# First gated input: order of sigmoids and forms, place of the third FFN's first weights, and block order of its first pair

## The chip, the cores and the metric

The kernel runs on one core of one Trainium2 chip. The metric is device time in microseconds; the median of three runs before the change is 2196.75 us (2195.62 to 2200.46). The engines in the profile are PE (matmuls) with PEld (its weight loads), DVE (VectorE), ACT (ScalarE), POOL (GpSimd) and SP (SyncE, which issues the weights' DMAs).

## The reference

Two layers act on a stream h of 512 tokens by 1024 features. Each layer runs a half-step SwiGLU FFN, a token mixer (retention in layer 0, forgetting attention in layer 1), a second half-step FFN, and a gated per-layer input; each takes a normed copy of h.

```
for i in range(DEPTH):
    h = h + 0.5 * swiglu(rmsnorm(h, nw[0]), ffn_w_in[i, 0], ffn_w_out[i, 0])
    hn = rmsnorm(h, nw[1])
    h = h + (retention(hn, ...) if i % 2 == 0 else forgetting_attention(hn, ...))
    h = h + 0.5 * swiglu(rmsnorm(h, nw[2]), ffn_w_in[i, 1], ffn_w_out[i, 1])
    gate = jax.nn.sigmoid(rmsnorm(h, nw[3]) @ ple_w_gate[i])
    h = h + gate * (p[i] @ ple_w_proj[i])
return rmsnorm(h, final_norm_w)
```

All is float32. The change is at the gated input of layer 0 and at the first FFN of layer 1, which follows it (the third of four FFNs, ffn index 2).

## The kernel before

**Layout.** h lies transposed in eight blocks h[0..7] of 128 features by 512 tokens. A product in float32 is made of three matmuls of rounded operands (`mm3`): weight high part times input high part, high times low, low times high. A "split" makes the parts: ScalarE casts the high part (L82), and the engine `W.low` subtracts it from the raw value for the low part (L83); `W.low` is VectorE in the FFNs and GpSimd inside `ple` (the gated input).

**Weights.** `W.plan` lists all weight blocks in order of use. `take` emits blocks up to two ahead (LOOKAHEAD): a DMA on SP into one of four raw buffers (`wraw`), then the split into one of three slots (`w8`). A raw buffer is free when both parts are made, a slot when PE's last product with it is done.

**The FFN's input half.** It is computed by a scheme of 2 by 2 quarters with seven products (Strassen's), on pairs of weight blocks: `Pair.q` and `Pair.r`. Most pairs need sums of quarters of the weights (`emit_sums`: adds at L151, splits at L82 and L83, buffers s12, s34 and a12 in a pool that each FFN opens) and sums and differences of the normed input's quarters, the "forms" (`Norm.quarters`: L381 to L412, whose casts and low parts are at L376 and L377). The first two pairs (PLAIN) are done plainly, from weights without sums: `plain(0)` and `plain(1)`, with 96 matmuls each at L526, 8 blocks by 2 halves of the tokens by 2 outputs by 3. They need the four quarters b11, b21, b12 and b22 of the forms; b12 (the "corner", L305 and L306) is made only for these, in buffers that the gates' inputs leave free.

**The gated input, `ple(0, ...)`.** For each block m PE makes the gate (`gates`: 24 matmuls) and the projected input (`added`: 6). Then `rest(m)`: VectorE scales the gate by the rows (L1112), ScalarE takes the sigmoid (L1113), VectorE multiplies (L1116) and adds to h[m] (L1117), and `nxt.block(m)` makes the next norm's forms of block m and adds its square into `acc` (L428, L432). After block 7 the sum of squares is split (L302, L303), and PE adds it over the features (L326, after the first plain pair) for the norm's scale.

**What sets the order.** PE's instructions stand in program order. Those of the other engines are ordered ahead of time by a planner that goes by readiness in its own cost model and by program order among what is ready; on the chip each engine then runs its own list strictly in order. The small tiles (`tmp`) have seven buffers.

Of the kernel before, what the change touches and what calls it, by code (L numbers as in the profile page):

```python
# [54 lines left out]
class Weights:  # L55
# [3 lines left out]
    def __init__(self, tc, raw_pool, pool):  # L59
        self.tc, self.nc, self.raw_pool, self.pool = tc, tc.nc, raw_pool, pool  # L60
        self.plan, self.ready, self.used = [], [], 0
        self.low = self.nc.vector
        self.limit, self.spare = None, []
        self.sum_pool, self.open_ffn, self.pairs_used = None, None, 0
        self.ahead, self.behind = 0, ()

# [18 lines left out]
    def chunk(self, src):  # L85
        n = src.shape[1]
        raw = self.load(src)
        if self.spare:
            tiles = [self.spare.pop(0)() for _ in range(4)]
            for i in range(2):  # L90
                self.split(raw[:, 512 * i : 512 * (i + 1)], tiles[i], tiles[2 + i])
            return Halves(tiles[0:2]), Halves(tiles[2:4])
        t = self.pool.tile([P, 2, 1024], F32R, name="w8")
        self.split(raw[:, :n], t[:, 0, :n], t[:, 1, :n], src)
        return t[:, 0, :], t[:, 1, :]
# [46 lines left out]
    def emit_sums_now(self):  # L142
        nc = self.nc
        pairs = [p for p in self.plan[: len(self.ready)] if isinstance(p, Pair) and p.ffn == self.open_ffn]
        for pair in pairs[: self.pairs_used + self.ahead]:
            if hasattr(pair, "s"):
                continue
            a11, a22 = pair.raw[:, 0:512], pair.raw[:, 512:1024]
            raw = self.load(pair.r)
            a12, a21 = raw[:, 0:512], raw[:, 512:1024]  # L150
            add = lambda o, p, q: nc.vector.tensor_tensor(out=o, in0=p, in1=q, op=ALU.add)  # L151
            fresh = lambda: self.sum_pool.tile([P, 512], F32, name="sums", bufs=4)
            s1, s2, s3, s4 = fresh(), fresh(), fresh(), fresh()
            pair.s = [self.sum_pool.tile([P, 2, 512], F32R, name=n, bufs=3) for n in ("s12", "s12", "s34", "s34")]
            pair.x = self.sum_pool.tile([P, 2, 512], F32R, name="a12")
            add(s1, a21, a22)
            add(s2, s1, a11)
            self.split(s1, pair.s[0][:, 0, :], pair.s[0][:, 1, :])
            self.split(s2, pair.s[1][:, 0, :], pair.s[1][:, 1, :])
            add(s4, s2, a12)  # L160
            add(s3, a21, a11)
            self.split(s4, pair.s[3][:, 0, :], pair.s[3][:, 1, :])
            self.split(s3, pair.s[2][:, 0, :], pair.s[2][:, 1, :])
            self.negated(a12, pair.x[:, 0, :], pair.x[:, 1, :], pair.r[:, 0:512])

    def open(self, ffn, pool):
        self.open_ffn, self.sum_pool, self.pairs_used, self.ahead, self.behind = ffn, pool, 0, 0, ()

    def begin(self, behind):
        self.ahead, self.behind = 2, behind  # L170
        self.emit_sums()
        self.behind = ()

    def take(self, src):
        assert self.plan[self.used] is src
        self.emit(self.used + 1 + LOOKAHEAD)
        self.used += 1
        return self.ready[self.used - 1]

# [8 lines left out]
def trunk(ctx, tc, a):  # L188
# [144 lines left out]
    class Norm:  # L333
        def __init__(self, gain, *pools):
            self.gain, self.hi, self.lo, self.acc = gain, [], [], None
            self.free = [p for p, n in pools for _ in range(n)]
            self.forms = [] if len(self.free) >= 28 else None
            self.new, self.left, self.extra = True, KB, None

        def unit(self):  # L340
            return unit(self.free.pop(0))
# [27 lines left out]
        def quarters(self, b):  # L369

            f = lambda ap: ap.bitcast(F32)
            c0, c1 = HALVES
            g = self.gain[:, b : b + 1]

            def part(raw, hi, lo, c):
                nc.scalar.copy(hi[:, c], raw[:, c])  # L376
                nc.vector.tensor_tensor(out=lo[:, c], in0=raw[:, c], in1=f(hi[:, c]), op=ALU.subtract)  # L377

            if b % 2 == 0:
                e, t = temp(), temp()  # L380
                nc.scalar.activation(e, h[b], AF.Identity, scale=g)  # L381
                if b // 2 == len(self.forms):
                    u = self.unit()
                    nc.scalar.copy(u[:, c0], e[:, c0])
                    nc.vector.tensor_tensor(out=u[:, c1], in0=e[:, c0], in1=f(u[:, c0]), op=ALU.subtract)
                    self.forms.append({"b11": (u[:, c0], u[:, c1])})
                ah, al = self.unit(), self.unit()
                nc.vector.tensor_tensor(out=t[:, c0], in0=e[:, c0], in1=e[:, c1], op=ALU.subtract)
                part(t, ah, al, c0)
                self.now = e, t, ah, al  # L390
                self.forms[b // 2].update({"t1": (ah[:, c0], al[:, c0]), "t2": (ah[:, c1], al[:, c1])})
            else:
                form = self.forms[b // 2]
                e, t, ah, al = self.now
                o, v = temp(), temp()
                nc.scalar.activation(o, h[b], AF.Identity, scale=g)
                if "b21" not in form:
                    oh, ol = self.unit(), self.unit()
                    part(o, oh, ol, slice(0, S))
                    form.update(b21=(oh[:, c0], ol[:, c0]), b22=(oh[:, c1], ol[:, c1]))  # L400
                if b == KB - 1 and self.extra:
                    for j, x in enumerate(self.forms):
                        u = unit(self.extra)
                        x["b12"] = u[:, c0], u[:, c1]
                        split(h[2 * j][:, c1], *x["b12"], self.gain[:, 2 * j : 2 * j + 1])
                nc.vector.scalar_tensor_tensor(
                    out=t[:, c1], in0=t[:, c0], scalar=-1.0, in1=o[:, c1], op0=ALU.mult, op1=ALU.subtract
                )
                part(t, ah, al, c1)
                bh, bl = self.unit(), self.unit()  # L410
                nc.vector.tensor_tensor(out=v[:, c0], in0=o[:, c1], in1=e[:, c1], op=ALU.subtract)
                nc.vector.scalar_tensor_tensor(  # L412
                    out=v[:, c1], in0=t[:, c1], scalar=-1.0, in1=o[:, c0], op0=ALU.mult, op1=ALU.subtract
                )
                part(v, bh, bl, slice(0, S))
                form.update(t3=(bh[:, c0], bl[:, c0]), t4=(bh[:, c1], bl[:, c1]))

        def square(self, b, ts_=slice(0, S), keep=False):

# [83 lines left out]
    def ffn(i, n, nxt, stack, apool, meanwhile=None):  # L503
# [7 lines left out]
        def plain(m, between=None):  # L511
# [1 line left out]
            ws = [W.take(ins[m].q), W.take(ins[m].r)]  # L513
            g, u = bank(), bank()
            order = [(k, t) for k in range(KB) for t in range(2)]
            if i:
                order.sort(key=lambda kt: kt[1])
            for at, (k, t) in enumerate(order):
                if at == 10 and between:
# [73 lines left out]

        done = PLAIN[i]
        whole = [plain(m) for m in range(done - 1)]
        W.begin(n.columns())

        def scaled():
            n.rows()
# [470 lines left out]
    def ple(l, n, nxt, phi, plo, parts=1):  # L1070

        w = S // parts
        with ExitStack() as pools:
# [12 lines left out]
            for part in range(parts):  # L1086
# [15 lines left out]
                def added(m):  # L1102
# [4 lines left out]
                        mm3(o, wp[0][:, ks], wp[1][:, ks], phi[k][:, ts_], plo[k][:, ts_], k == 0, k == 1)  # L1107
                    return o

                def rest(m, g, o):  # L1110
                    t1, t2, hm = temp()[:, :w], temp()[:, :w], h[m][:, ts_]
                    nc.vector.tensor_tensor(out=t1, in0=g, in1=n.r[:, ts_], op=ALU.mult)  # L1112
                    nc.scalar.activation(t1, t1, AF.Sigmoid)  # L1113
                    if parts > 1 and m == KB - 1:
                        nc.scalar.activation(warm, t1[:, 0:1], AF.Sqrt)
                    nc.vector.tensor_tensor(out=t2, in0=o, in1=t1, op=ALU.mult)  # L1116
                    nc.vector.tensor_tensor(out=hm, in0=hm, in1=t2, op=ALU.add)  # L1117
                    if parts == 1:
                        nxt.block(m)
                    else:  # L1120
                        nxt.new = m == 0
                        nxt.square(m, ts_, keep=m == KB - 1)
                        nc.gpsimd.tensor_scalar(out=hm, in0=hm, scalar1=fw[:, m : m + 1], scalar2=None, op0=ALU.mult)

                m = 0
                if part == 0:
# [16 lines left out]
                    if parts > 1:  # L1143
                        rest(4, gs[4], added(4))
                        m = 5
                while m < KB:
                    g = gates((m,))[0]
                    rest(m, g, added(m))
# [2 lines left out]
                    if part > 0 and m == 4:  # L1151
                        final(diag, slice(ts_.start - w, ts_.start))
                    m += 1
            W.low = nc.vector
            if parts > 1:
                final(final_scale(nxt, ts_), ts_)

    def final_scale(n, ts_):
# [37 lines left out]
    norms = [Norm(nw(i), *where[i]) for i in range(8)] + [Norm(fw)]  # L1196
    norms[4].extra = norms[6].extra = ua
    norms[2].extra = ud
    first = W.emit_parts(((0, 1), (1, 2), (2, 4)))
    next(first)  # L1200
    load_x(1, 2)
# [133 lines left out]
```

## Time and profile before

| what | value |
|---|---|
| median of three runs | 2196.75 us |
| the profiled execution | 2196.75 us, of which the span is 2195.0 |
| PE busy | 2140.7 us (98%) |
| VectorE busy | 1455.9 us (66%) |
| ScalarE busy | 1201.0 us (55%) |
| GpSimd busy | 466.3 us (21%) |
| gated input's last gate done on PE | at about 1165.3 us |
| first and second plain pair of the third FFN start on PE | 1166.65 us and 1192.66 us |
| first product from weight sums (L493) | 1205.64 us |

A timeline row gives start, duration, engine, line, operation, output and input tile, count, and in brackets the idle time before it with the instruction that ended it. A group's row gives count, then busy time, mean in ns, then idle time before and its releasers. Durations of neighbours on one engine overlap by some 0.08 us, since an instruction's end is drained while the next begins.

### The profile page before, as it was taken

Reading aid. Unit: us, or ns where it says so; the run is one execution under the profiler, and the core shown is the slowest. Engines: PE = TensorE matmul, PEld = TensorE weight load, DVE = VectorE, ACT = ScalarE, POOL = GpSimd, SP = SyncE. Lnnn points to the kernel's source line nnn. Section 1 sums busy time; section 2 is a strip of 40 time slices with the busy share of each in tenths; the row PEclk is TensorE's granted clock in tenths of the full one; section 3 lists DMA queues with packets and bytes.
Section 4 is the critical chain, followed back from the end, with each engine's and each line's share of the span. In section 5 each row is a group of like instructions: output and inputs, shape, how many; then the busy total and the mean of one; then the engine's idle time right before and its main releaser. Section 6 shows DMA issues by size and latency. Waiting matters only on the chain.

```text
span 2195.0 us, 34450 instructions
## 1 busy us (share of the span) xinstructions
PE 2140.7 (98%) x13525; PEld 1927.3 (88%) x13525; DVE 1455.9 (66%) x2631; ACT 1201.0 (55%) x2027; POOL 466.3 (21%) x352
## 2 busy tenths in 40 slices
PE   8999999999999999999998999999999999999997
PEld 7898997888888798989887999898788899999987
DVE  8686766352533777867758677775675696877765
ACT  7464553433333664736546556464787774655544
POOL 0010103434444010101141011012334200100055
PEclk9999999999999999999999999999999999999999
DMA  5465562222222254746423556463622144655631
GB/s 183 120 175 137 141 158 96 84 98 77 88 86 77 78 144 125 176 132 154 125 87 96 130 146 162 130 165 107 152 86 87 68 124 113 164 153 139 154 106 40
DMA packets 85315, 267.08 MB, mean 122 GB/s; under 512 B 9360, under 2 KB 12944, under 8 KB 85152
## 3 DMA queue, kind: packets, MB, share of 16 engines
q1 hardware_dynamic: 63328, 209.78, 28.2%
q0 software_dynamic: 20592, 54.01, 14.6%
q8 instruction: 106, 1.74, 0.3%
q10 hardware_dynamic: 1232, 1.09, 0.1%
q14 instruction: 57, 0.47, 0.1%
HBM read 262.71 MB, written 2.13 MB: 121 GB/s over the span
## 4 chain that ended last, share of the span: by engine, by line
PE 83%; DVE 6%; ACT 4%; issue 4%; DMA 2%; POOL 1%; SPq 0%; DVEq 0%; ACTq 0%; POOLq 0%
PE bank L493 33%; PE bank L314 13%; PE bank L312 13%; PE bank L313 13%; PE bank L526 3%; PE bank L685 2%; PE bank L684 2%; PE bank L686 2%; DMA wraw<-in_ffn_w_in 1%; DVE w L83 1%; POOL w L83 1%; ACT p L988 1%; ACT w L82 1%; ACT p L990 1%; DVE tlo L303 1%
## 5 line engine op out<-in xcount | busy, mean ns | idle before, releaser
L82 ACT CAST w<-wraw 128x1024 fp32r<-128x1024 f32 (+1 forms) x242 | 245.6, 1022 | 421.2 <-PE bank L314 255.3
L314 PE MATMUL bank<-unit_a,w 128*128 128x512 f32 x736 | 287.2, 390 | 4.3 <-DVE w L83 2.6
L312 PE MATMUL bank<-unit_a,w 128*128 128x512 f32 x736 | 288.4, 392 | 1.9 <-ACT w L82 1.6
L313 PE MATMUL bank<-unit_a,w 128*128 128x512 f32 x736 | 286.7, 389 | 0.2 <-DVE unit_a L303 0.2
L83 POOL TENSOR_TENSOR w<-wraw,w 128x1024 fp32r<-128x1024 f32 x93 | 226.3, 2436 | 271.9 <-ACT w L82 259.4
L82 ACT CAST s<-sums 128x512 fp32r<-128x512 f32 x320 | 191.6, 617 | 153.9 <-DVE sums L151 101.9
L314 PE MATMUL bank<-unit_d,w 128*128 128x512 f32 (+1 forms) x712 | 267.5, 376 | 4.6 <-DVE w L83 4.6
L312 PE MATMUL bank<-unit_d,w 128*128 128x512 f32 (+1 forms) x712 | 268.6, 377 | 3.2 <-ACT w L82 1.6
L313 PE MATMUL bank<-unit_d,w 128*128 128x512 f32 (+1 forms) x712 | 267.6, 376 | 1.8 <-DVE unit_d L303 1.8
L83 DVE TENSOR_TENSOR s<-sums,s 128x512 fp32r<-128x512 f32 x320 | 214.0, 685 | 77.8 <-ACT s L82 77.3
L122 POOL DMA_DIRECT2D a<-in_ffn_w_in x80 | 70.1, 876 | 640.8 <-ACT a L121 460.5
L83 DVE TENSOR_TENSOR w<-wraw,w 128x1024 fp32r<-128x1024 f32 (+1 forms) x149 | 175.7, 1184 | 17.7 <-ACT w L82 17.6
L493 PE MATMUL bank<-unit_b,s 128*128 128x256 f32 x880 | 184.5, 276 | 0.7 <-DVE bank L548 0.7
L493 PE MATMUL bank<-unit_d,s 128*128 128x256 f32 x1140 | 178.3, 276 | 0.0
L587 DVE SCALAR_TENSOR_TENSOR tmp<-bank,rows 128x512 f32<-128x512 f32 x96 | 66.0, 689 | 166.4 <-PE bank L314 165.0
L493 PE MATMUL bank<-unit_a,s 128*128 128x256 f32 x1260 | 175.0, 276 | 1.4 <-ACT unit_a L376 0.9
L314 PEld LDWEIGHTS bank<-unit_a,w 128*128 128x128 f32 x736 | 138.1, 188 | 35.5 <-DVE w L83 4.3
L312 PEld LDWEIGHTS bank<-unit_a,w 128*128 128x128 f32 x736 | 138.2, 188 | 32.2 <-ACT w L82 3.5
L313 PEld LDWEIGHTS bank<-unit_a,w 128*128 128x128 f32 x736 | 138.2, 188 | 28.4 <-DVE unit_a L303 0.5
L314 PEld LDWEIGHTS bank<-unit_d,w 128*128 128x128 f32 x712 | 133.9, 188 | 30.3 <-DVE w L83 6.6
L312 PEld LDWEIGHTS bank<-unit_d,w 128*128 128x128 f32 x712 | 134.0, 188 | 30.2 <-ACT w L82 3.3
L493 PEld LDWEIGHTS bank<-unit_a,s 128*128 128x128 f32 x1260 | 158.0, 188 | 1.8 <-ACT unit_a L376 1.1
(268 smaller groups left out, 4772.2 us busy)
## 6 DMA issues: line engine op xcount, KB each, us to landing
wraw<-in_ffn_w_in SPq DMA_DIRECT2D x174, 512.0 KB, 4.3
wraw<-in_ffn_w_out SPq DMA_DIRECT2D x64, 512.0 KB, 4.8
w<-in_ffn_w_in POOLq DMA_DIRECT2D x56, 512.0 KB, 5.3
a<-in_ffn_w_in POOLq DMA_DIRECT2D x80, 256.0 KB, 6.1
wraw<-in_ffn_w_out SPq DMA_DIRECT2D x32, 384.0 KB, 4.3
wraw<-in_ret_qk SPq DMA_DIRECT2D x16, 512.0 KB, 3.4
wraw<-in_ret_v SPq DMA_DIRECT2D x16, 512.0 KB, 3.6
wraw<-in_ret_g SPq DMA_DIRECT2D x16, 512.0 KB, 3.5
```

What stands on the lines that cost most here:

```text
L82: self.nc.scalar.copy(hi, raw)
L83: self.low.tensor_tensor(out=lo, in0=raw, in1=hi.bitcast(F32), op=ALU.subtract)
L122: self.nc.gpsimd.dma_start(out=lo, in_=src, accum_op=ALU.add)
L312: nc.tensor.matmul(out, wh, xh, start=first, stop=False)
L313: nc.tensor.matmul(out, wh, xl, start=False, stop=False)
L314: nc.tensor.matmul(out, wl, xh, start=False, stop=last)
L493: add = lambda w, x, start, stop: nc.tensor.matmul(out, w, x, start=start, stop=stop, skip_group_check=True)
L526: nc.tensor.matmul(o[:, HALVES[t]], x[:, ks], y, start=k == t == q == 0, stop=k == KB - 1 and q == 2, skip_group_check=True,)
L587: nc.vector.scalar_tensor_tensor(out=t1, in0=o, scalar=-0.5, in1=n.r, op0=ALU.mult, op1=ALU.mult)
L684: nc.tensor.matmul(os[t], xh, wh[:, js], start=k == 0, stop=False)
L685: nc.tensor.matmul(os[t], xh, wl[:, js], start=False, stop=False)
L686: nc.tensor.matmul(os[t], xl, wh[:, js], start=False, stop=k == KB - 1)
```

## The change

Four things are done at the first gated input, and at the FFN after it.

1. **Order in `ple`.** With `parts == 1` (layer 0) `rest` calls the new `step`: scaled gate and sigmoid of block m come first, then the next norm's work for block m-1, then multiply and add for block m. The work for block 7 follows after the loop.
2. **Corners.** For the norm with `early` (norms[4], the third FFN's) the corners of forms 0 to 2 are emitted before block 6's forms and that of form 3 after them, instead of all four within block 7's.
3. **Weights.** From the gate of block 4 on, `W.look` is four instead of two, and the two blocks of the third FFN's first pair are split into four tiles of the sum pool (three s34, one a12) instead of two slots of `w8`. As `take` emits further ahead, the second pair's blocks are emitted inside `ple` too, where `W.low` is GpSimd.
4. **Third FFN.** Its plain pairs run through blocks 0 to 5 for the first half of the tokens, blocks 0 to 5 for the second, then blocks 6 and 7 for both. The first weight sums to be emitted are queued on VectorE behind the last instruction of block 7's forms (`n.last`); for the other FFNs nothing is queued behind anything. (Before, `begin` named two instructions but emitted no sums, since no pair with sums had been loaded by then, and forgot them.)

```
 def chunk(self, src):
     raw = self.load(src)
+    if id(src) in self.placed:
+        hi, lo = (t.rearrange("p a c -> p (a c)") for t in self.placed.pop(id(src))())
+        self.split(raw, hi, lo)
+        return hi, lo
...
+def place_first(self, pair):
+    tile = lambda n, b: self.sum_pool.tile([P, 2, 512], F32R, name=n, bufs=b)
+    self.placed[id(pair.q)] = lambda: (tile("s34", 3), tile("s34", 3))
+    self.placed[id(pair.r)] = lambda: (tile("s34", 3), tile("a12", 2))
...
 def begin(self, behind):
     self.ahead, self.behind = 2, behind
     self.emit_sums()
-    self.behind = ()
...
-    self.emit(self.used + 1 + LOOKAHEAD)
+    self.emit(self.used + 1 + self.look)
...
+def corner(self, js):
+    c0, c1 = HALVES
+    for j in js:
+        u = unit(self.extra)
+        self.forms[j]["b12"] = u[:, c0], u[:, c1]
+        split(h[2 * j][:, c1], *self.forms[j]["b12"], self.gain[:, 2 * j : 2 * j + 1])
...
-    if i:
+    if i == 2:
+        order.sort(key=lambda kt: (kt[0] >= KB - 2, kt[1]))
+    elif i:
         order.sort(key=lambda kt: kt[1])
...
-W.begin(n.columns())
+n.columns()
+W.begin((n.last,) if n.early else ())
...
+def step(m, g, o):
+    t1 = temp()
+    nc.vector.tensor_tensor(out=t1, in0=g, in1=n.r, op=ALU.mult)
+    nc.scalar.activation(t1, t1, AF.Sigmoid)
+    if m == KB - 1 and nxt.early:
+        nxt.corner(range(KB // 2 - 1))
+    if m:
+        nxt.block(m - 1)
+    if m == KB - 1 and nxt.early:
+        nxt.corner((KB // 2 - 1,))
+    t2 = temp()
+    nc.vector.tensor_tensor(out=t2, in0=o, in1=t1, op=ALU.mult)
+    nc.vector.tensor_tensor(out=h[m], in0=h[m], in1=t2, op=ALU.add)
...
+if parts == 1:
+    W.look = LOOKAHEAD + 2
+    W.place_first(ffn_src[2][0][0])
 while m < KB:
     g = gates((m,))[0]
     rest(m, g, added(m))
...
-W.low = nc.vector
-if parts > 1:
+W.low, W.look = nc.vector, LOOKAHEAD
+if parts == 1:
+    nxt.block(KB - 1)
+else:
     final(final_scale(nxt, ts_), ts_)
...
+norms[4].early = True
```

More of the change, by code (lines that the diff above doesn't have):

```diff
@@ L63, in __init__ @@
         self.limit, self.spare = None, []
+        self.look, self.placed = LOOKAHEAD, {}
         self.sum_pool, self.open_ffn, self.pairs_used = None, None, 0
@@ L147, in emit_sums_now @@
                 continue
+            self.behind = ()
             a11, a22 = pair.raw[:, 0:512], pair.raw[:, 512:1024]
@@ L154, in emit_sums_now @@
             pair.s = [self.sum_pool.tile([P, 2, 512], F32R, name=n, bufs=3) for n in ("s12", "s12", "s34", "s34")]
-            pair.x = self.sum_pool.tile([P, 2, 512], F32R, name="a12")
+            pair.x = self.sum_pool.tile([P, 2, 512], F32R, name="a12", bufs=2)
             add(s1, a21, a22)
@@ L337, in __init__ @@
             self.forms = [] if len(self.free) >= 28 else None
-            self.new, self.left, self.extra = True, KB, None
+            self.new, self.left, self.extra, self.early = True, KB, None, False
         def unit(self):
@@ L376, in part @@
                 nc.scalar.copy(hi[:, c], raw[:, c])
-                nc.vector.tensor_tensor(out=lo[:, c], in0=raw[:, c], in1=f(hi[:, c]), op=ALU.subtract)
+                return nc.vector.tensor_tensor(out=lo[:, c], in0=raw[:, c], in1=f(hi[:, c]), op=ALU.subtract)
             if b % 2 == 0:
@@ L400, in quarters @@
                     form.update(b21=(oh[:, c0], ol[:, c0]), b22=(oh[:, c1], ol[:, c1]))
[L401 to L405, printed above, removed]
+                if b == KB - 1 and self.extra and not self.early:
+                    self.corner(range(KB // 2))
                 nc.vector.scalar_tensor_tensor(
@@ L414, in quarters @@
                 )
-                part(v, bh, bl, slice(0, S))
+                self.last = part(v, bh, bl, slice(0, S))
                 form.update(t3=(bh[:, c0], bl[:, c0]), t4=(bh[:, c1], bl[:, c1]))
+        def corner(self, js):
[4 more added lines that the diff above has]
+                split(h[2 * j][:, c1], *self.forms[j]["b12"], self.gain[:, 2 * j : 2 * j + 1])
         def square(self, b, ts_=slice(0, S), keep=False):
@@ L1108, in added @@
                     return o
+                def step(m, g, o):
[11 more added lines that the diff above has]
+                    nc.vector.tensor_tensor(out=h[m], in0=h[m], in1=t2, op=ALU.add)
                 def rest(m, g, o):
+                    if parts == 1:
+                        step(m, g, o)
+                        return
                     t1, t2, hm = temp()[:, :w], temp()[:, :w], h[m][:, ts_]
@@ L1113, in rest @@
                     nc.scalar.activation(t1, t1, AF.Sigmoid)
-                    if parts > 1 and m == KB - 1:
+                    if m == KB - 1:
                         nc.scalar.activation(warm, t1[:, 0:1], AF.Sqrt)
@@ L1117, in rest @@
                     nc.vector.tensor_tensor(out=hm, in0=hm, in1=t2, op=ALU.add)
[L1118 to L1123, printed above, removed]
+                    nxt.new = m == 0
+                    nxt.square(m, ts_, keep=m == KB - 1)
+                    nc.gpsimd.tensor_scalar(out=hm, in0=hm, scalar1=fw[:, m : m + 1], scalar2=None, op0=ALU.mult)
                 m = 0
@@ L1153, in ple @@
                     m += 1
-            W.low = nc.vector
-            if parts > 1:
+            W.low, W.look = nc.vector, LOOKAHEAD
+            if parts == 1:
+                nxt.block(KB - 1)
+            else:
                 final(final_scale(nxt, ts_), ts_)
```

## The prediction

> **What bounds the kernel now.** I read the page first, then the matmul engine's waits, then its timeline where the longest wait stands.
>
> ```profile
> span 2195.0 us, 34450 instructions
> PE 2140.7 (98%) x13525; PEld 1927.3 (88%) x13525; DVE 1455.9 (66%) x2631; ACT 1201.0 (55%) x2027; POOL 466.3 (21%) x352
> ```
>
> PE is busy for 98% of the span, so the change can only return what PE loses near the place it touches. The profiled execution took 2196.75 us: the span and 1.75 us around it. That is also the median of the three runs (2195.62 to 2200.46), so differences on the span are subtracted from 2196.75.
>
> The longest wait of PE in the whole kernel stands at the first gated input, between the per-layer input (L1112 to L1117) and the third FFN's first pair (L526). PE's timeline there, start and duration:
>
> ```profile
> 1166.65 0.51 PE L526 MATMUL bank<-unit_b,w 128*128 128x256 f32 x3
> 1172.86 0.80 PE L526 MATMUL bank<-unit_b,w 128*128 128x256 f32 x2 [5.70 <-ACT w L82]
> 1176.06 3.14 PE L526 MATMUL bank<-unit_b,w 128*128 128x256 f32 x13 [2.40 <-POOL w L83]
> 1179.00 4.26 PE L526 MATMUL bank<-unit_d,w 128*128 128x256 f32 x24
> 1184.59 0.39 PE L526 MATMUL bank<-unit_c,w 128*128 128x256 f32 x1 [1.33 <-ACT unit_c L376]
> 1185.39 0.86 PE L526 MATMUL bank<-unit_c,w 128*128 128x256 f32 x5 [0.42 <-DVE unit_c L377]
> 1191.85 0.95 PE L326 MATMUL bank<-ones_r,tmp 128*128 128x2 f32 x8
> 1194.20 1.82 PE L526 MATMUL bank<-unit_b,w 128*128 128x256 f32 x13 [0.70 <-DVE w L83]
> 1195.86 3.04 PE L526 MATMUL bank<-unit_d,w 128*128 128x256 f32 x24
> 1198.74 0.88 PE L526 MATMUL bank<-unit_c,w 128*128 128x256 f32 x6
> 1205.64 0.64 PE L493 MATMUL bank<-unit_b,w 128*128 128x256 f32 x4
> ```
>
> In the undisturbed second pair 24 matmuls take 1198.74 - 1195.86 = 2.88 us, 0.12 us each. The first pair's 96 would take 11.5 us; they take 1191.85 - 1166.65 = 25.2. So 13.7 us are lost here, and 0.70 us in the second pair: 14.4 us is all there is to win. The losses, in order: the second weight block's high part (5.70) and low part (2.40), matmuls at half rate (24 in 1184.59 - 1.33 - 1179.00 = 4.3 us), and block 7's forms (1.33 + 0.42). The half rate is the granted clock, the third figure from the right of each row (busy, clock, DMA share, GB/s):
>
> ```profile
> 1168.00:1170.00 2.00, 0.00 (x0) 1.00 0.61 236
> 1170.00:1172.00 2.00, 0.00 (x0) 0.89 0.00 0
> 1180.00:1182.00 2.00, 2.00 (x12) 0.55 0.41 135
> 1182.00:1184.00 2.00, 1.26 (x11) 1.00 0.34 135
> ```
>
> PE went idle at 1167.16. The clock fell about 4.4 us later (a mean of 0.89 over 1170 to 1172 is 0.44 us at 0.50) and was whole again at about 1181.9, 9.0 us after the restart at 1172.86.
>
> **What is late behind the weights.** Were the weights there, the stall would go to the forms of block 7, made by the chain L1112 (times rows), L1113 (sigmoid), L1116, L1117 (update of h), then scaling, casts and L377. The groups of VectorE from the first L1112 to block 7's L377, with busy time, mean, and idle time before:
>
> ```profile
> 1128.30:1185.40 57.10, 47.67 (x73) 0.91 0.26 86
> L1117 DVE TENSOR_TENSOR hall<-hall,tmp 128x512 f32<-128x512 f32 x8 | 12.1, 1510 | 0.2
> L1116 DVE TENSOR_TENSOR tmp<-bank,tmp 128x512 f32<-128x512 f32 x8 | 5.5, 685 | 3.8 <-ACT tmp L1113 3.8
> L306 DVE SCALAR_TENSOR_TENSOR unit_a<-hall,small,unit_a 128x256 fp32r<-128x256 f32 x4 | 4.0, 998 | 0.0
> L377 DVE TENSOR_TENSOR unit_b<-tmp,unit_b 128x512 fp32r<-128x512 f32 x2 | 3.0, 1491 | 0.0
> L377 DVE TENSOR_TENSOR unit_d<-tmp,unit_d 128x512 fp32r<-128x512 f32 x4 | 2.7, 682 | 0.0
> L406 DVE SCALAR_TENSOR_TENSOR tmp<-tmp 128x256 f32<-128x256 f32 x4 | 1.7, 424 | 2.4 <-ACT tmp L396 2.4
> L388 DVE TENSOR_TENSOR tmp<-tmp 128x256 f32<-128x256 f32 x4 | 1.7, 422 | 2.4 <-ACT tmp L381 2.4
> L83 DVE TENSOR_TENSOR w<-wraw,w 128x1024 fp32r<-128x1024 f32 x1 | 1.2, 1214 | 0.0
> L151 DVE TENSOR_TENSOR sums<-wraw 128x512 f32<-128x512 f32 x1 | 0.7, 693 | 0.6 <-DMA wraw<-in_ffn_w_in 0.6
> L151 DVE TENSOR_TENSOR sums<-sums,wraw 128x512 f32<-128x512 f32 x1 | 0.7, 684 | 0.0
> L83 DVE TENSOR_TENSOR s<-sums,s 128x512 fp32r<-128x512 f32 x1 | 0.7, 681 | 0.0
> ```
>
> VectorE is busy 47.7 of 57.1 us: it is the bound of this stretch, and it starts the last L1112 at 1177.62, 12 us after PE has left that gate for the last products of added() (unit_c, from 1165.29):
>
> ```profile
> 1165.29 0.39 PE L312 MATMUL bank<-unit_c,w 128*128 128x512 f32 x1
> 1177.62 0.68 DVE L1112 TENSOR_TENSOR tmp<-bank,rows 128x512 f32<-128x512 f32 x1
> 1172.73 0.47 DVE L306 SCALAR_TENSOR_TENSOR unit_a<-hall,small,unit_a 128x256 fp32r<-128x256 f32 x1
> 1163.67 0.68 DVE L1116 TENSOR_TENSOR tmp<-bank,tmp 128x512 f32<-128x512 f32 x1
> 1164.39 2.80 DVE L1117 TENSOR_TENSOR hall<-hall,tmp 128x512 f32<-128x512 f32 x1
> 1164.24 2.40 POOL L83 TENSOR_TENSOR w<-wraw,w 128x1024 fp32r<-128x1024 f32 x1 [4.12 <-ACT w L82]
> L83 POOL TENSOR_TENSOR w<-wraw,w 128x1024 fp32r<-128x1024 f32 x8 | 19.9, 2492 | 32.2 <-ACT w L82 28.2 <-issue 4.0
> ```
>
> Part of this busy time is no work. L1117 took 2.80 us instead of 0.69 exactly while GpSimd ran a weight's low part (1164.24 to 1166.64); an instruction that reads a PSUM bank, like L1116, kept its 0.68. From the groups: L1117 12.1 - 8 x 0.69 = 6.6, L377 on unit_b 3.0 - 1.36 = 1.6, L306 4.0 - 4 x 0.47 = 2.1. That is 10.3 us blocked, by six GpSimd instructions (the eight less two in the idle start): 1.7 us each. Foreign work is L83 w, L151 twice and L83 s: 3.3. Own work is then 47.7 - 10.3 - 3.3 = 34.1, idle 9.4.
>
> By the Trainium skill, page "SBUF — State Buffer", section "Who interferes with whom", a VectorE instruction with two SBUF inputs and a GpSimd instruction that reads SBUF lock each other out for a whole instruction. The trace agrees (2.80 against 0.69 us), and the rule speaks against this change; what it would give is the last rival.
>
> **The change part by part.**
>
> *Weights.*
>
> ```profile
> 1171.78 1.03 ACT L82 CAST w<-wraw 128x1024 fp32r<-128x1024 f32 x1
> ```
>
> This is the cast that PE waited for. q and r of the first pair go to the sum buffers (s34, a12), idle until the first sums, so they need no slot of the weight pool, and two more blocks are emitted ahead. Nothing is added: the same DMA, the same cast (1.03 us) and low part (2.40). The cast of r was the 5.70 us wait; its raw block can land while gates run. The second pair's q and r find slots earlier too, so its 0.70 us wait goes. The price: their low parts move from VectorE (L83 w, 1.2) to GpSimd, inside this stretch: eight blocking instructions instead of six. On GpSimd and ScalarE q and r now come before or among the splits of the last gates; a gate that waits 2.4 us for that costs nothing, since PE idles longer than this before block 7.
>
> *Sigmoids first.* L1112 and L1113 of block m stand before the forms of block m-1, so L1112 (0.68) can fill the wait for the scaled copy before L388 and L406 (2.4 + 2.4 over six places), and L1116 finds its sigmoid done. Of the idle time before the first L1116, that for the first sigmoid stays:
>
> ```profile
> 1131.58 0.69 DVE L1116 TENSOR_TENSOR tmp<-bank,tmp 128x512 f32<-128x512 f32 x1 [2.56 <-ACT tmp L1113]
> ```
>
> Bounds: filled gaps save 6 x 0.60 = 3.6, L1116's other waits 3.8 - 2.56 = 1.2 and the DMA wait before L151 0.6 go as well, which leaves 9.4 - 5.4 = 4.0 us; 9.4 if the order on the engines stays as it is (it follows when buffers come free, which the trace doesn't show for the new order). I take 5.0, nearer the filled case, because the filler is 0.68 us and the gaps 0.79.
>
> *Sums behind the last block.* L151 and L83 s leave the stretch: 3.3 us with L83 w. What waits now is pair 2's sums, behind them ScalarE's casts of s, and behind those SP's next loads. Eight sum instructions of 0.7 us fit between block 7 and the first product that needs them, one whole pair (11.5 us) later; the s34 tiles come free at the end of the first pair, and the products that read s34 come last. I cost this at nothing; without that cover it would be up to 5.6 us.
>
> *Block order.* With blocks 6 and 7 last in both halves, PE can do 78 of 96 matmuls before it needs block 7, and only 18 stand behind it (53 stood behind it before: from 1185.39 to 1191.85).
>
> *Corners* (L306) move ahead of block 6: four small instructions, the same count; inside the own work.
>
> **The sum.** X is the end of block 7's first L377: before, 1185.3. Now X = 1128.3 + 34.1 own + 5.0 idle + 8 x 1.7 = 13.7 blocked = 1181.1. Bounds: 34.1 + 4.0 + 10.3 (the two extra ones fall elsewhere) gives 1176.7; 34.1 + 9.4 + 8 x 2.4 gives 1191.0. PE reaches block 7 at 1166.65 + 78 x 0.12 = 1176.0 and waits 5.1 us, close to the 4.4 us after which the clock fell, though waits for corners may cut the idle time up. So two ends for X = 1181.1. The rest, L326 to L493 at 1205.64, took 13.8 less the 0.70 wait: 13.1. Full clock: L326 needs the halves of the sum of squares, 2.7 us behind X as before:
>
> ```profile
> 1184.66 0.68 DVE L377 TENSOR_TENSOR unit_c<-tmp,unit_c 128x512 fp32r<-128x512 f32 x1
> 1187.40 0.68 DVE L303 TENSOR_TENSOR tmp<-acc,tmp 128x512 fp32r<-128x512 f32 x1
> ```
>
> 1183.8 + 13.1 = 1196.9, which is 8.7 us before 1205.64. Half clock: 18 x 0.24 = 4.3 to 1185.4, half rate until 1190.1 loses another 2.35, end 1200.9: 4.7 us gained. I take the middle, 6.7: **2190.0 us**.
>
> By the Trainium skill, page "TensorE: Matmul & The Clock Gate", section "What's actually happening", an idle window of about 3.4 us brings the half clock; the trace showed it 4.4 us after the idle began. By that rule the gain would be the 4.7.
>
> **The rivals.** (1) *The chain keeps PE's pace.* All gaps filled, the extra GpSimd work elsewhere: X = 1176.7, L326 at 1179.4, end 1192.5, gain 13.1: 2183.6. For it: the chain starts 12 us late and the gaps are of the right size. Against: the locks stay. 18%. (2) *The order doesn't help.* The planned order of VectorE stays or what is saved goes to the two new locks: X = 1185.3, 1189.6 after 18 slow matmuls, end 1189.6 + 13.1 + 2.35 = 1205.05: 2196.2. For it: 10.3 us of locks, which no reordering takes away. 25%. (3) *Slower by the port.* Each of eight GpSimd instructions blocks its whole 2.4 us and no gap is filled: X = 1191.0, PE restarts cold, end 1210.75, 5.1 us later than before: 2201.9. From X = 1185.9 on the change loses. For it: L1117 at 2.80; against: L1112 and L1116 read PSUM and run beside the lock. 12%. The lock rule named above, taken for each instruction in full, leads to this case.
>
> **How the numbers follow.** The forecast, X from 1178 to 1183.5, has 45% and its own range 2185 to 2193.5. A measurement here tells about 0.2%, 4.4 us, from no change. Faster by more: rival 1 and nine tenths of the forecast, 0.58; within: the rest and rival 2, 0.30; slower: 0.12. The range takes in rivals 1 and 2 and leaves out most of 3: 2182.5 to 2197.5.
>
> **What would show it.** Right: L526 no longer waits for L82 or L83 at the first pair; PE's last wait there is for L376 or L377 on unit_c with at most 18 matmuls behind it; eight GpSimd L83 beside stretched L1117; no L151 before block 7; L1112 of an odd or even block inside the former gap before L388 or L406. Wrong: L326 waiting long, L493 waiting for s (sums late), L312 to L314 waiting for GpSimd by more than 5 us, or X after 1185.9.

## The result, and the profile after

The changed kernel takes 2190.22 us (median of 17 runs, 2187.24 to 2196.26), the kernel before 2197.42 us (17 runs, 2194.89 to 2200.46): a ratio of 0.9969 with a 95% interval of 0.9962 to 0.9977, which is some 6.8 us of 2197.42 (the medians are 7.2 apart). The prediction said 2190.0 us and 6.7 us faster.

The profiled execution of the changed kernel took 2193.35 us, more than the median. It reached the gated input later than the profile before: its first scaled gate starts at 1130.92 us instead of 1128.32. The two profiles differ from the first 50 us on (granted clock 0.93 against 0.97), long before the code that was changed, and the kernels of the experiments start that gate anywhere between 1127.4 and 1135.1. So all that follows is measured inside one stretch: from the first scaled gate on VectorE to the first product from weight sums on PE. Before, it is 1205.64 - 1128.32 = 77.3 us.

Lines have moved: L1112 is now L1131, L1116 is L1140, L1117 is L1141, L526 is L543, L326 is L337, L493 is L508, L377 is L388, L83 is L84, L306 is L317, L388 is L399, L406 is L414, L303 is L314, L151 is L157, L82 is L83. In the experiments they move by a few more; the tiles keep their names. The page's head, and PE's timeline after (start, duration, in brackets the idle time and what ended it):

```profile
span 2191.5 us, 34456 instructions
PE 2142.5 (98%) x13525; PEld 1927.9 (88%) x13525; DVE 1454.5 (66%) x2629; ACT 1202.4 (55%) x2027; POOL 472.6 (22%) x354
```

```profile
1169.18 0.75 PE L543 MATMUL bank<-unit_b,s 128*128 128x256 f32 x5
...
1175.13 0.74 PE L543 MATMUL bank<-unit_a,s 128*128 128x256 f32 x4 [1.43 <-DVE unit_a L317]
...
1178.25 0.74 PE L543 MATMUL bank<-unit_a,s 128*128 128x256 f32 x4 [1.44 <-DVE unit_a L317]
...
1183.26 0.39 PE L543 MATMUL bank<-unit_c,s 128*128 128x256 f32 x1 [1.32 <-ACT unit_c L387]
1183.98 0.39 PE L543 MATMUL bank<-unit_c,s 128*128 128x256 f32 x1 [0.34 <-DVE unit_c L388]
...
1187.57 0.94 PE L337 MATMUL bank<-ones_r,tmp 128*128 128x2 f32 x7 [1.06 <-DVE tmp L314]
1188.37 2.98 PE L543 MATMUL bank<-unit_b,w 128*128 128x256 f32 x18
...
1194.26 0.88 PE L543 MATMUL bank<-unit_a,w 128*128 128x256 f32 x6
...
1201.88 0.64 PE L508 MATMUL bank<-unit_b,w 128*128 128x256 f32 x4
```

The stretch is 1201.88 - 1130.92 = 71.0 us, 6.4 less. No wait for a weight is left in the two pairs (5.70, 2.40 and 0.70 before). In their place stand two waits for corners (L317), block 7's forms (1.32 + 0.34) and a new one, 1.06 us, for the sum of squares at L337. The clock didn't fall in the first pair. It fell in the second, where 36 matmuls took 1194.26 - 1188.37 = 5.9 us instead of 4.3. The third figure from the right of each window is the clock:

```profile
1188.00:1190.00 2.00, 2.00 (x18) 0.97 0.00 0
1190.00:1192.00 2.00, 2.00 (x11) 0.50 0.14 35
1192.00:1194.00 2.00, 2.00 (x13) 0.67 0.83 266
```

VectorE's groups from the first scaled gate to X, the end of block 7's first low part, first the window (busy time behind its length), then busy, mean, idle before:

```profile
1130.90:1183.95 53.05, 46.33 (x68) 1.00 0.31 105
```

```profile
L1141 DVE TENSOR_TENSOR hall<-hall,tmp 128x512 f32<-128x512 f32 x8 | 10.6, 1320 | 0.0
L414 DVE SCALAR_TENSOR_TENSOR tmp<-tmp 128x256 f32<-128x256 f32 x4 | 5.8, 1441 | 1.8 <-ACT tmp L407 1.8
L1140 DVE TENSOR_TENSOR tmp<-bank,tmp 128x512 f32<-128x512 f32 x8 | 5.4, 680 | 2.6 <-ACT tmp L1132 2.6
L317 DVE SCALAR_TENSOR_TENSOR unit_a<-hall,small,unit_a 128x256 fp32r<-128x256 f32 x4 | 3.3, 852 | 0.0
L399 DVE TENSOR_TENSOR tmp<-tmp 128x256 f32<-128x256 f32 x4 | 3.0, 746 | 1.9 <-ACT tmp L392 1.9
L84 DVE TENSOR_TENSOR w<-wraw,w 128x1024 fp32r<-128x1024 f32 x1 | 1.2, 1208 | 0.0
L396 DVE TENSOR_TENSOR unit_d<-tmp,unit_d 128x256 fp32r<-128x256 f32 x2 | 0.8, 418 | 0.4 <-ACT unit_d L395 0.4
L84 POOL TENSOR_TENSOR w<-wraw,w 128x1024 fp32r<-128x1024 f32 x8 | 20.3, 2538 | 19.7 <-ACT w L83 15.7 <-issue 4.0
L84 POOL TENSOR_TENSOR a<-wraw,s 128x1024 fp32r<-128x1024 f32 x1 | 2.9, 2894 | 0.0
L84 POOL TENSOR_TENSOR s<-wraw,s 128x1024 fp32r<-128x1024 f32 x1 | 2.9, 2886 | 0.0
```

Blocked time: L1141 10.6 - 8 x 0.69 = 5.1, L414 5.8 - 4 x 0.42 = 4.1, L317 3.3 - 4 x 0.47 = 1.4, L399 3.0 - 4 x 0.42 = 1.3: together 11.9 us, by eight GpSimd instructions (ten less two at the idle start). Idle 2.6 + 1.8 + 1.9 + 0.4 = 6.7, foreign work 1.2 (L84 w, a weight of the third pair), own work the rest, 33.2. X is 53.0 us behind the first scaled gate; before it was 57.0.

### The profile page after: what moved, and what is told of

It is laid out like the page before. It is cut to its first block, busy times and chain, and to the rows that moved or that the text cites. A ratio compares the mean times of both kernels' runs of the same rounds, so it can differ in the third digit from the quotient of the medians.

```text
span 2191.5 us, 34456 instructions
## 1 busy us (share of the span) xinstructions
PE 2142.5 (98%) x13525; PEld 1927.9 (88%) x13525; DVE 1454.5 (66%) x2629; ACT 1202.4 (55%) x2027; POOL 472.6 (22%) x354
## 4 chain that ended last, share of the span: by engine, by line
PE 85%; DVE 6%; ACT 4%; DMA 2%; issue 2%; POOL 1%; SPq 0%; ACTq 0%; DVEq 0%; POOLq 0%
PE bank L508 33%; PE bank L325 14%; PE bank L323 14%; PE bank L324 13%; PE bank L543 4%; PE bank L703 2%; PE bank L702 2%; PE bank L704 2%; DMA wraw<-in_ffn_w_in 1%; ACT p L1006 1%; DVE w L84 1%; ACT p L1008 1%; ACT w L83 1%; DVE tlo L314 1%; PE bank L337 0%
## 5 line engine op out<-in xcount | busy, mean ns | idle before, releaser
L83 ACT CAST w<-wraw 128x1024 fp32r<-128x1024 f32 (+1 forms) x240 | 243.4, 1021 | 420.0 <-PE bank L325 254.9
L84 POOL TENSOR_TENSOR w<-wraw,w 128x1024 fp32r<-128x1024 f32 x93 | 226.8, 2442 | 259.3 <-ACT w L83 246.8
L83 ACT CAST s<-sums 128x512 fp32r<-128x512 f32 x320 | 191.8, 617 | 153.4 <-DVE sums L157 107.4
L84 DVE TENSOR_TENSOR s<-sums,s 128x512 fp32r<-128x512 f32 x320 | 214.1, 685 | 75.8 <-ACT s L83 75.3
L84 DVE TENSOR_TENSOR w<-wraw,w 128x1024 fp32r<-128x1024 f32 (+1 forms) x147 | 173.3, 1184 | 19.5 <-ACT w L83 19.3
L508 PE MATMUL bank<-unit_b,s 128*128 128x256 f32 x880 | 184.4, 276 | 0.7 <-DVE bank L565 0.7
L508 PE MATMUL bank<-unit_d,s 128*128 128x256 f32 x1140 | 178.4, 276 | 0.0
L508 PE MATMUL bank<-unit_a,s 128*128 128x256 f32 x1260 | 175.0, 276 | 1.4 <-ACT unit_a L387 0.9
L508 PEld LDWEIGHTS bank<-unit_a,s 128*128 128x128 f32 x1260 | 158.0, 188 | 1.8 <-ACT unit_a L387 1.1
```

The source lines that it names most:

```text
L83: self.nc.scalar.copy(hi, raw)
L84: self.low.tensor_tensor(out=lo, in0=raw, in1=hi.bitcast(F32), op=ALU.subtract)
L508: add = lambda w, x, start, stop: nc.tensor.matmul(out, w, x, start=start, stop=stop, skip_group_check=True)
```

## The experiments

Each kernel is the kernel after with one thing changed, but for the first, which is the kernel before with one part of the change, and for two that combine two changes ("VectorE and DMA" and "all on VectorE, no weights part"). "Stretch" and X are taken from each one's own profile, a single execution; X counts from the first scaled gate. The ratio is to the kernel before, timed on the same chip.

| kernel | X us | stretch us | ratio (95% interval) |
|---|---|---|---|
| before | 57.0 | 77.3 | 1 |
| after | 53.0 | 71.0 | 0.9969 (0.9962 to 0.9977) |
| weights alone | 60.8 | 82.1 | 1.0018 (1.0005 to 1.0031) |
| without weights | 50.9 | 69.6 | 0.9968 (0.9957 to 0.9980) |
| old block order | 53.0 | 74.3 | 0.9980 (0.9969 to 0.9990) |
| old sigmoid order | 59.8 | 76.7 | 0.9997 (0.9988 to 1.0007) |
| sums free | 57.5 | 76.7 | 0.9993 (0.9983 to 1.0002) |
| pair's low parts by DMA | 51.0 | 67.5 | 0.9962 (0.9947 to 0.9977) |
| pair's low parts on VectorE | 50.1 | 68.4 | 0.9960 (0.9946 to 0.9975) |
| all low parts on VectorE | 48.9 | 66.5 | 0.9952 (0.9935 to 0.9969) |
| VectorE and DMA | 46.3 | 62.8 | 0.9947 (0.9929 to 0.9966) |
| all on VectorE, no weights part | 47.3 | 66.5 | 0.9954 (0.9937 to 0.9970) |
| after again | 52.9 | 69.4 | 0.9969 (0.9957 to 0.9980) |

### The weights alone

To the kernel before are added the placement in the sum buffers (`place_first`, the branch in `chunk`) and the longer look:

```
+if parts == 1:
+    W.look = LOOKAHEAD + 2
+    W.place_first(ffn_src[2][0][0])
 while m < KB:
     g = gates((m,))[0]
```

> The kernel before with part 3 alone (first pair in the sum buffers, look of four). Measure: the stretch from the first scaled gate on VectorE to the first product from weight sums on PE, 77.3 us before and 71.0 after. Theory T (block 7's forms, end X of the chain on VectorE, and the matmuls that stand behind X set the end): the 5.7 and 2.4 us waits for the weights go, but X stays where it was or moves back by the locks of two more GpSimd instructions (up to 3 us), and with the old block order 54 matmuls stand behind it, at half clock after an idle time of 10 us and more: stretch 77 to 84, kernel same or up to 7 us slower. Rival W (the weights were the stall, the rest is decoration): 8.1 + 0.7 us less, stretch about 69, kernel 8 us faster.

The stretch came to 82.1 us and the kernel was slower. PE's waits in it, sum, count and longest:

```profile
PE bank L537 <- ACT unit_d L395: 6.2, 1, 6.2
PE bank L537 <- ACT unit_c L387: 2.5, 1, 2.5
PE bank L325 <- POOL w L84: 1.7, 1, 1.7
PE bank L323 <- ACT w L83: 1.4, 1, 1.4
```

PE no longer waits for r; it waits 6.2 and 2.5 us for the forms instead. The chain is later than before (X 60.8 against 57.0), and a gate waits 1.4 and 1.7 us for its own weight's cast and low part, which come late with ScalarE's list. Rival W falls: taking the longest wait of the kernel away, by itself, made it a little slower. The two more GpSimd instructions are only a part of that. With the longer look six instructions of the first weight sums stand on VectorE ahead of X, where the kernel before had three:

```profile
L156 DVE TENSOR_TENSOR sums<-wraw 128x512 f32<-128x512 f32 x2 | 3.6, 1791 | 0.0
L84 DVE TENSOR_TENSOR s<-sums,s 128x512 fp32r<-128x512 f32 x2 | 2.9, 1458 | 0.0
L156 DVE TENSOR_TENSOR sums<-sums,wraw 128x512 f32<-128x512 f32 x2 | 1.4, 682 | 0.0
```

They take 7.9 us with the blocking, 4.1 without (6 x 0.69). In all, VectorE is blocked for 13.9 us, against 10.3 before.

### Without the weights

```
-if parts == 1:
-    W.look = LOOKAHEAD + 2
-    W.place_first(ffn_src[2][0][0])
```

> The kernel after without part 3 (old slots, look of two; sigmoids first, corners, block order and sums as after). T: PE still waits for the cast and low part of r until about 9 us behind the last gate and then runs 78 matmuls, the first half of them slowly, so the weights decide again: stretch 74 to 77, most of the gain lost. X itself should come 1 to 3 us earlier than in the kernel after, with two GpSimd locks fewer. Rival F (the forms alone decide): stretch 71 or less, no loss. Rival W: as before, 77.3.

The stretch is 69.6 us, no longer than after, and the ratio is the same. This went against theory T. PE's timeline and ScalarE's cast of r in this kernel, and the last wait on ScalarE ahead of that cast in the kernel before:

```profile
1165.96 0.51 PE L543 MATMUL bank<-unit_b,w 128*128 128x256 f32 x3
1167.60 0.50 PE L543 MATMUL bank<-unit_b,w 128*128 128x256 f32 x2 [1.12 <-ACT w L83]
1170.62 3.06 PE L543 MATMUL bank<-unit_b,w 128*128 128x256 f32 x13 [2.53 <-POOL w L84]
...
1186.07 1.82 PE L543 MATMUL bank<-unit_b,w 128*128 128x256 f32 x13 [1.29 <-DVE w L84]
```

```profile
1166.52 1.03 ACT L83 CAST w<-wraw 128x1024 fp32r<-128x1024 f32 x1
```

```profile
1167.22 0.72 ACT L396 ACTIVATE tmp<-hall,small 128x512 f32<-128x512 f32 x1 [3.06 <-DVE hall L1117]
```

The wait of 5.70 us has shrunk to 1.12 without any weight being placed elsewhere. The cast of r stands 1166.52 - 1127.86 = 38.7 us behind the first scaled gate; before it stood 1171.78 - 1128.32 = 43.5 behind. No idle time stands directly before the cast on ScalarE in either, so it waited for no slot and no transfer: the wait for r was not a lack of buffers. ScalarE runs its list in order. In the kernel before, that list had stood 3.06 us for an update of h on VectorE (the L1117 that took 2.80 us beside GpSimd), and nine instructions filled the time from 1167.22 to the cast at 1171.78. When the chain runs earlier, so does the cast. The waits that remain here (1.12 + 2.53 + 1.29) sum to 4.9 us, PE's waits in the kernel after to 5.6. Without the two extra GpSimd instructions of the weights part X is 2.1 us earlier than after: VectorE is blocked for 7.2 us instead of 11.9, and idle for 8.7 instead of 6.7.

### The old order of blocks

```
-if i == 2:
-    order.sort(key=lambda kt: (kt[0] >= KB - 2, kt[1]))
-elif i:
+if i:
     order.sort(key=lambda kt: kt[1])
```

> The kernel after with the old order of blocks in the third FFN's plain pairs (all blocks for the first half of the tokens, then all for the second). T: X unchanged, but 54 instead of 18 matmuls stand behind it: 3 us later at full clock, up to 7 us if the one long idle time lowers the clock: stretch 74 to 78. Rival W (weights alone): no change, 71.

As T said: X is the same 53.0 us, the stretch 74.3, 3.4 more. (The kernel's time says less: the interval of 0.9980 overlaps that of 0.9969.) The waits moved to the forms, which PE now needs with 54 matmuls left to do:

```profile
PE bank L541 <- ACT unit_d L395: 4.7, 1, 4.7
PE bank L541 <- ACT unit_c L387: 2.1, 1, 2.1
```

### The old order of sigmoids

```
 nc.scalar.activation(t1, t1, AF.Sigmoid)
 if m == KB - 1 and nxt.early:
-    nxt.corner(range(KB // 2 - 1))
-if m:
-    nxt.block(m - 1)
-if m == KB - 1 and nxt.early:
-    nxt.corner((KB // 2 - 1,))
+    nxt.corner(range(KB // 2))
 t2 = temp()
 nc.vector.tensor_tensor(out=t2, in0=o, in1=t1, op=ALU.mult)
 nc.vector.tensor_tensor(out=h[m], in0=h[m], in1=t2, op=ALU.add)
+nxt.block(m)
...
-if parts == 1:
-    nxt.block(KB - 1)
-else:
+if parts > 1:
     final(final_scale(nxt, ts_), ts_)
```

> The kernel after with the old order of the gated input (multiply, add and forms of block m before the scaled gate of block m+1; corners ahead of block 7's forms). T: VectorE's gaps before the scaled copies come back (6.7 us idle after, 9.4 before), X 2 to 4 us later, stretch 73 to 75. Rival P (the order on the engines is set by readiness, and locks by GpSimd absorb what the order saves): X within 1 us, stretch 70.5 to 72.

Nearly all of the gain is gone: X 6.8 us later, stretch 76.7, both beyond what T had said (2 to 4 us, 73 to 75). VectorE's groups with idle time before them:

```profile
L1136 DVE TENSOR_TENSOR tmp<-bank,tmp 128x512 f32<-128x512 f32 x8 | 5.5, 685 | 3.6 <-ACT tmp L1132 3.5
L396 DVE TENSOR_TENSOR unit_b<-tmp,unit_b 128x256 fp32r<-128x256 f32 x2 | 2.9, 1426 | 0.8 <-ACT unit_b L395 0.8
L414 DVE SCALAR_TENSOR_TENSOR tmp<-tmp 128x256 f32<-128x256 f32 x4 | 1.7, 426 | 2.8 <-ACT tmp L407 2.8
L399 DVE TENSOR_TENSOR tmp<-tmp 128x256 f32<-128x256 f32 x4 | 1.7, 424 | 2.4 <-ACT tmp L392 2.4
```

They sum to 9.6 us against 6.7 after: 2.9 of the 6.8 us. The rest is mostly blocking, which by the same reckoning as above comes to some 14.5 us instead of 11.9, under as many GpSimd instructions. VectorE and GpSimd in the middle of the chain:

```profile
1155.19 2.44 DVE L396 TENSOR_TENSOR unit_b<-tmp,unit_b 128x256 fp32r<-128x256 f32 x1 [0.82 <-ACT unit_b L395]
1157.55 2.65 DVE L388 TENSOR_TENSOR unit_d<-tmp,unit_d 128x256 fp32r<-128x256 f32 x1
```

```profile
1154.93 2.41 POOL L84 TENSOR_TENSOR w<-wraw,w 128x1024 fp32r<-128x1024 f32 x1 [2.33 <-ACT w L83]
1157.30 2.62 POOL L84 TENSOR_TENSOR a<-wraw,s 128x1024 fp32r<-128x1024 f32 x1
```

Two half-size instructions of 0.42 us take 2.44 and 2.65 under two GpSimd instructions back to back, and the scaled gate, which reads PSUM, stands behind them in VectorE's list, at 1160.13. Rival P falls. The edit also makes the four corners in one go again; where they stand (part 2 of the change) was not tested by itself.

### The sums free

```
-W.begin((n.last,) if n.early else ())
+W.begin(())
```

> The kernel after, but the first weight sums aren't queued behind block 7's forms. T: adds and splits of the sums go in front of block 7 on VectorE again, 2 to 4 instructions of 0.7 us and perhaps a wait for a transfer: X 1.5 to 3.5 us later, stretch (71.0 after, 77.3 before) 72 to 75. Rival (s34 tiles that hold the first pair keep the sums back anyway): 71.

X is 4.5 us later, stretch 76.7. VectorE's groups of the sums that now stand ahead of X:

```profile
L157 DVE TENSOR_TENSOR sums<-sums,wraw 128x512 f32<-128x512 f32 x3 | 2.1, 693 | 0.1
L157 DVE TENSOR_TENSOR sums<-wraw 128x512 f32<-128x512 f32 x3 | 2.0, 681 | 0.0
L84 DVE TENSOR_TENSOR s<-sums,s 128x512 fp32r<-128x512 f32 x2 | 3.4, 1676 | 0.0
```

Eight instructions, 7.5 us with the blocking, where I had expected two to four and 1.5 to 3.5 us. The tiles that hold the first pair did not keep them back; that rival falls.

### The price of GpSimd

Three kernels take low parts away from GpSimd. First, the four of the first two pairs go by a negated copy and an accumulating DMA; then the same four on VectorE; then every one of the gated input on VectorE:

```
-self.split(raw, hi, lo)
+self.split(raw, hi, lo, src)
...
-if self.low is None and src is not None:
+if src is not None and (self.low is None or id(src) in self.by_other):
     self.negated(raw, hi, lo, src)
...
+W.by_other = {id(s) for x in ffn_src[2][0][0:2] for s in (x.q, x.r)}
```

> The kernel after, but the low parts of the first two pairs' four blocks are made by a negated copy on ScalarE and an accumulating DMA instead of a GpSimd subtraction. Theory L (GpSimd's subtractions block VectorE's two-input instructions, 12.0 us in eight of them in the kernel after): the four that go take 5 to 6 us of blocking with them, X comes 4 to 5 us earlier (no earlier than PE's own pace allows, 13.6 us behind the last gate's L1131), stretch 65 to 68, kernel 3 to 6 us faster than the kernel after. Rival A (the long VectorE instructions have another cause, or ScalarE's four more instructions of 1 us take the place): stretch 70 to 72.

> The kernel after with the same four low parts on VectorE itself (1.2 us each). L: 5 to 6 us of blocking are traded for 4.8 us of VectorE's own work: X within 1.5 us, stretch 69.5 to 71.5. If VectorE's long instructions had nothing to do with GpSimd, X would be 4.8 us later, stretch 75 or more.

In the second, the branch makes the low part with `nc.vector.tensor_tensor` in place of `negated`. The third has only this:

```
-W.low = nc.gpsimd
+W.low = nc.gpsimd if parts > 1 else nc.vector
```

> The kernel after with every low part of the first gated input on VectorE, none on GpSimd. L: no L1117 or forms instruction is stretched any more (L1141 at 0.69 each, 10.6 us for eight of them in the kernel after); 12.0 us of blocking are traded for nine times 1.2 = 10.8 us of own work, X within 2 us, stretch 69 to 72. If GpSimd isn't the cause, the stretched instructions stay and X is about 10 us later, stretch 78 and more.

By DMA: stretch 67.5 as expected, but X only 2.0 us earlier instead of 4 to 5, and the kernel's ratio (0.9962) is not clearly better than that of the kernel after, where 3 to 6 us had been expected. The blocking did go, from 11.9 to 4.7 us. But VectorE is idle for 11.9 us instead of 6.7, most of it in one wait. That wait was for a copy on ScalarE, whose list had stood on a transfer shortly before:

```profile
1170.58 0.42 DVE L415 SCALAR_TENSOR_TENSOR tmp<-tmp 128x256 f32<-128x256 f32 x1 [6.43 <-ACT tmp L408]
```

```profile
1166.36 0.62 ACT L126 CAST a<-wraw 128x512 fp32r<-128x512 f32 x1 [4.54 <-DMA wraw<-in_ffn_w_in]
```

The same cast waits 0.53 us in the kernel after. So ScalarE took part of the place, as rival A had it, though by this wait in its list; how much the four more copies add by their own length was not measured. The same four on VectorE: X 2.9 us earlier, better than the trade I had priced. All on VectorE: X 4.1 us earlier, stretch 66.5, again better than the trade. VectorE's groups of this last kernel:

```profile
L84 DVE TENSOR_TENSOR w<-wraw,w 128x1024 fp32r<-128x1024 f32 x9 | 11.0, 1219 | 4.1 <-ACT w L83 4.1
L1141 DVE TENSOR_TENSOR hall<-hall,tmp 128x512 f32<-128x512 f32 x8 | 5.5, 684 | 0.0
L414 DVE SCALAR_TENSOR_TENSOR tmp<-tmp 128x256 f32<-128x256 f32 x4 | 1.7, 418 | 0.8 <-ACT tmp L407 0.8
```

With GpSimd gone from the stretch, L1141 takes 684 ns in all eight cases (1320 on average after) and L414 418 ns (1441 after). Theory L holds. By the Trainium skill, page "SBUF — State Buffer", section "Who interferes with whom", whichever of the two engines issues first holds the port that they share for its whole instruction, and the other blocks. The runs agree in both directions, since GpSimd's own 2.40 us became 2.9 for the two placed blocks above, each of which began 0.6 us before an L1141 of VectorE ended.

### VectorE and DMA together

The gates' low parts on VectorE and the pairs' by DMA, both edits above:

> The kernel after with no subtraction on GpSimd in the first gated input: the gates' low parts on VectorE, the four low parts of the first two pairs by a negated copy on ScalarE and an accumulating DMA. If VectorE's own work and the blocking by GpSimd are all that holds X: against the kernel with every low part on VectorE (X 48.9 us behind the first scaled gate, stretch 66.5) four times 1.2 us go, X at 44 to 46.5, PE reaches block 7 without a wait (37.4 + 9.4 = 46.8), and the sum of squares is ready when PE asks for it: stretch 63 to 64.5, kernel 12 to 14 us faster than before and 6 to 8 faster than after. Rival (ScalarE's four more copies and the DMAs take VectorE's place, or the planner orders worse): X 48 or later, stretch 66 to 68.

X is 46.3 us, as expected, and the stretch 62.8, just below. All that PE waits for in the stretch, and one wait of the whole span:

```profile
PE bank L338 <- DVE tmp L315: 1.1, 1, 1.1
...
PE bank L509 <- ACT tmp L565: 4.5, 3, 1.8
```

The second sums to 2.0 us after; so some of what the stretch wins is given back in the FFN products behind it, and this kernel's median is 4.7 us below that of the kernel after on the same chip (2191.92), not 6 to 8. This is the lowest ratio of the study: 2187.24 us against 2199.39 for the kernel before on the same chip, 0.9947 (0.9929 to 0.9966). Its lead over the kernel after is likely but not certain, since their runs overlap (2183.03 to 2193.97 and 2189.51 to 2197.35), and it can't be told from the kernel with all low parts on VectorE (0.9952).

### All on VectorE, without the weights part

The edit of `W.low` above, on the kernel without the weights:

> The kernel with every low part of the gated input on VectorE, without part 3 (old slots, look of two). The study so far: without part 3 the kernel after was no slower (stretch 69.6 against 71.0), because part 3 brings two GpSimd instructions into the chain and the wait for r's cast shrank by itself when ScalarE's list ran earlier. Here no GpSimd instruction is in the chain, so part 3's price is gone. If it is worth something by itself, PE waits here 1.5 to 3 us for r's parts and about 1 us in the second pair, and block 7 isn't the bound: stretch 66 to 69 against 66.5. If part 3 is worth nothing in either form: 64 to 66.5, since two of VectorE's 1.2 us instructions leave the chain.

```profile
PE bank L543 <- DVE w L84: 2.7, 2, 1.4
```

Stretch 66.5, the same as with the weights part, though X is 1.6 us earlier (47.3 against 48.9): PE waits for r's and the second pair's low parts instead of for block 7. That is the border between the two outcomes named ahead of the run, and the ratios (0.9954 and 0.9952) are the same, so it stays open whether the weights part is worth something once GpSimd is gone. In the kernel of VectorE and DMA (X 46.3), which has the weights part, both kinds of wait are gone. That kernel without the weights part was not run.

### The kernel after again

> The kernel after, unchanged, beside the two others on the same chip. Stretch 70 to 72, 5 to 8 us faster than the kernel before.

The stretch is 69.4 us, 1.6 less than in the first profile, slightly below the expected 70; the kernel is 7.5 us faster than the kernel before on that chip, as expected. X and the waits for corners and block 7 are the same to 0.2 us. The clock fell at another place:

```profile
1184.00:1188.00 4.00, 4.00 (x26) 0.64 0.00 0
```

Here the slow matmuls are the last of the first pair and cover the wait for the sum of squares, which is not there. So 1.5 us of a stretch is a matter of where the low clock falls, and differences of that size between two stretches in the table are not to be read as an effect.

## Why the prediction was right

**X.** Predicted 34.1 own + 5.0 idle + 13.7 blocked = 52.8 us behind the first scaled gate; measured 33.2 + 6.7 + 11.9 + 1.2 foreign = 53.0. That the total is right to 0.2 us is luck: its terms err both ways. Blocking was eight instructions as counted, at 1.5 us each instead of 1.7. The idle time was nearer the middle of its bounds (4.0 to 9.4) than the value taken. The foreign term was set to nothing, but a weight's low part (L84 w) still stands between block 7's update and its forms.

**Behind X.** The 18 matmuls stood behind X as said. But "L326 needs the halves of the sum of squares, 2.7 us behind X" was too early: PE took L337 up again 3.6 us behind X, after a wait of 1.06 us. The half clock was given two ends for the gain, 8.7 and 4.7, because of one idle time of 5.1 us. The idle time was cut up by the corners, as the text allowed, and the clock didn't fall at block 7; it fell a little later in the second pair, for 1.6 us. The measured 6.4 us of the stretch lies between the two ends for another reason than the one given, and the profile after again gives 7.9. So it is luck, too, that the middle of two cases, of which neither came about, was so near.

**The block order** did what was said: taking it back costs 3.4 us with X unchanged.

**The weights: the step that failed.** The prediction put the 5.70 us wait down to the missing slot ("so they need no slot of the weight pool") and made its removal the opening of the sum. The runs show that the wait was the same lateness of the chain, through ScalarE's list: the kernel without that part is as fast. Alone, the part costs 0.0018 of the time, and the longer look, which lets more of the sums in front of X, has its share in that. Rival 2's reason, that the saving goes to two new locks, describes this part well: without it VectorE is blocked for 4.7 us less, and X is 2.1 us earlier.

**The sigmoids first** were priced by the gaps, 9.4 - 5.0 = 4.4 us; without them X is 6.8 us later. Of that 2.9 is idle time; the term left out is that another order meets GpSimd's instructions at other places, which in the run above cost two half-size instructions 2 us each and some 2.6 us in all.

**The sums behind the last block** were priced at 2.1 of the 3.3 us (the rest was a weight's low part); without the order X is 4.5 us later. That they cost nothing later held, as far as the timeline shows: no product waits for s in the two pairs or at the first product behind them.

**The rivals.** The chain at PE's pace (X 48.4 us behind the first scaled gate, 13.1 us gained) did not come about in this kernel, for the reason given against it: the locks stay. With the locks gone, X at 46.3 is that case, and the kernel took 12.2 us less than the kernel before on the same chip. The slower end by the port (X 62.7 behind, 5.1 us lost) came about in size with the weights alone (X 60.8, stretch 4.8 longer), but not in the way described: the eight GpSimd instructions blocked 1.7 us each and not 2.4, and sums ahead of X did the rest.

## What to carry to other kernels

The longest wait in a profile can be a symptom: before giving the late instruction a buffer of its own, look at what stands ahead of it in its engine's list, and why that is late. Two engines that block each other can make an instruction moved to the idle one cost more than it saves; here a subtraction of 1.2 us on the busy VectorE was cheaper than one of 2.4 us on an idle GpSimd, which blocked VectorE for 1.5 us on average. Where a chain ends late, order the consumer so that as little as possible stands behind its last product: here 18 matmuls instead of 54.

## What the runs showed of the hardware

A half-size VectorE instruction of 0.42 us took 2.44 and 2.65 us under GpSimd, twice in a row. Each ended 0.3 us behind the GpSimd instruction that it ran into, so what it lost was the rest of that instruction, not a share of its own length. And the clock does not only fall after one long idle time (4.4 us before): in the kernel after no single wait of PE was longer than 1.44 us, yet it fell to 0.50 at about 1190, some 16 us after the first of them began.
